# Joint pooling weights, pooled tiles stored as split, sooner input splits, and one exponential a head in a tuned encoder layer

## The chip, the cores and the metric

The kernel runs on one core of a Trainium2 chip. The core has five engines with in-order instruction queues of their own: TensorE (PE in the profile; PEld is its weight load), VectorE (DVE), ScalarE (ACT), GpSimd (POOL) and SyncE (SP), which here only issues DMA transfers. The metric is the device time of one execution, in microseconds; lower is better. Before the change it is 1769.13 us, the median of three runs (1767.67 to 1769.21).

## The reference

One encoder layer is applied to two requests with shared weights: 512 positions ("prompt") and 1024 positions ("sample"), of 1024 channels. All data are float32.

```python
a = rmsnorm(h) ; z = a @ w_in              # 1024 -> 512 q + 128 k + 128 v + 512 u
q, k = rotary(rmsnorm(q)), rotary(rmsnorm(k))   # 8 q heads, 2 k heads, of 64
o_attn = softmax(q @ k.T / 8) @ v          # every position sees all of its request
# pooling, for each of four groups of 128 channels, windows 2, 4, 8, 16:
d = window_mean(u) - u
o_pool = (d @ w_pool[group]) * pool_scale
h = h + concat(o_attn, o_pool) @ w_out     # 512 + 512 rows -> 1024
h = h + square(relu(rmsnorm(h) @ w_up)) @ w_down        # 1024 -> 4096 -> 1024
h = h + sigmoid(rmsnorm(h) @ w_ple_gate) * (p @ w_ple_proj)
y = rmsnorm(h)
```

The pooled part of the output is a product of three: d (positions x 128), w_pool (128 x 128) with its scale, and 128 rows of w_out.

## The kernel before, in words

The 1536 positions are 12 tiles of 128 (t = 0 to 11; the prompt is tiles 0 to 3) and 3 chunks of 512 (c = 0, 1, 2). Nearly every float32 operand of a matmul is **split** in two parts: a rounded high part (float32r, written by a copy) and the remainder (a subtraction). A product is then three matmuls (`three`: high-high, high-low, low-high). So every new operand costs a copy on ScalarE and a subtraction on VectorE or GpSimd. All working tiles on chip come from one pool of 49 equal slots; a slot holds 1056 numbers for each of the 128 partitions; a full tile of 1024 columns is 512 KB.

The order of instructions on TensorE, ScalarE, VectorE and GpSimd is the order of the code. Loads go through SyncE's single queue, in the order of the code too, each no earlier than the matmul issued just before it; stores stand in the same queue. A load or store that waits holds back all that are behind it.

**Stage 1, input projection** (0 to about 200 us). For each tile t, `mm_k(t, k)` runs the nine matmuls of one of the eight blocks k of 128 input channels into the PSUM tile z (two buffers). Between these steps stands everything else by hand: after k = 2 `split_x` and `stat_x` of the next x tile, after k = 3 `rotary` of the tile before (VectorE), after k = 6 `turn_qk`, which transposes the rotated q and k (PSUM tiles qp, kp), copies them to qs and ks on ScalarE, subtracts on VectorE and stores qs to DRAM (qs_d). After k = 4 a finished pooled tile goes through `pool_product`. A table `first`, keyed by (t, k), holds further work: in tiles 10 and 11 the loads of the pooling rows of w_out (wor4 to wor7), their splits (wo4 to wo7), and the first scores of attention. `pool_step` advances the window sums on GpSimd, which end in a split tile dhl for each chunk c and group g (12 in all). `pool_product` multiplies it by the split w_pool (three 512-column matmuls into py), scales and splits the result (y), and stores it to DRAM (yT_d).

The rotary uses four tables, tabq and tabk, products of the gains gq, gk and the cosines and sines (csr). GpSimd makes them at the start; GpSimd also computes the norm factor hr of each tile's heads (`rstd_of`). csr stands in the load queue behind x2 and several small constants.

**Attention** (about 200 to 560 us) is a pipeline over steps `at`; each step takes one of four heads of a unit (tile t, group g). `Unit.score` makes S (128 x 512 for the prompt, 128 x 1024 for the sample) and its row maximum nm on VectorE; `soften` the exponential on ScalarE with a running sum; `norm` the reciprocal rr on VectorE and the multiplication on GpSimd; `turn` transposes 128-column blocks of four heads (tp); `split` makes the split pt (ScalarE cast, VectorE subtraction); `weigh` multiplies with v. For the sample, `soften` makes two exponentials of 512 columns, each with its sum, and `norm` adds the two sums on VectorE first (L455):

```python
if self.nc == 2:
    ve.tensor_tensor(rr, self.sums[:, j, 0:1], self.sums[:, j, 1:2], op=ALU.add)
    ve.reciprocal(rr, rr)
```

Each step also takes one or two pieces from a list of **fillers** (`fill`): matmuls that depend on little, first the pooled part of the output projection (`pool_out`, which reads the stored pooled tiles yb and the weights wo4 to wo7, PSUM tile pp), then the heads' part (`heads_out`, po). A dictionary `extras`, keyed by the step, holds what is left of stage 1: turn_u and the rotary of tile 11 and turn_qk of tiles 10 and 11. In the later part of attention "chores" also run (`make_m`), which make the MLP's inputs on GpSimd, VectorE and ScalarE.

**MLP** (about 560 to 1560 us): seven products in place of eight for each pair of blocks (PSUM tiles px, py, pz, pq up; pd down); the sums of weight blocks made for chunk 0 are stored (kept_d) and loaded again for chunks 1 and 2. Chores between the products prepare what follows. One of them, `gating(0)`, runs near the MLP's end: for a = 0 to 3 it loads a quarter of the residual h (from hl_d), squares it and makes the split gated input hg (`gate_in`), sums the squares (`total`), and stores hg (hg_d). The generator `staged` runs the stages of the four items as a pipeline, the last stage of the oldest item first:

```python
yield from staged(range(4), fetch, square, total, keep)
```

**Gate and output** (about 1560 us to the end): products with w_ple_gate (pg) and w_ple_proj (pj), the sigmoid, the final norm and the stores.

## Time and profile before

| what | value |
|---|---|
| median of three runs | 1769.13 us (1767.67 to 1769.21) |
| the profiled execution, its own time | 1772.11 us |
| its span (first to last instruction) | 1770.3 us |
| granted clock of TensorE, mean | 0.992 |
| TensorE, matmuls: busy | 1727.3 us, 98%, 11692 instructions |
| TensorE, weight loads: busy | 1574.4 us, 89% |
| VectorE busy | 1287.1 us, 73%, 1786 instructions |
| GpSimd busy | 1078.4 us, 61%, 933 instructions |
| ScalarE busy | 906.9 us, 51%, 1730 instructions |
| DMA moved | 391.78 MB, 221 GB/s over the span |

The busy shares are means over stages with different limits, so views of single stretches are needed beside them. In the lists of groups, `out<-in` names the tile written and the tiles read, then the shapes, a count, the busy time and the mean in ns of one, and the idle time just before these instructions with what ended it. In the timeline, a row gives start, duration, engine, source line, operation and tiles, and in brackets the wait that stood ahead of it and its releaser. The clock is the share of full speed that TensorE was granted.

### The profile page before, as it was taken

What the parts mean: (1) busy time and instruction counts of PE and PEld (TensorE: products, weight loads), DVE (VectorE), ACT (ScalarE), POOL (GpSimd) and SP (SyncE); (2) the same over time, 40 slices, a digit from 0 to 9 for tenths busy, and PEclk for the clock granted to TensorE, in tenths of its full rate; (3) what the DMA queues carried; (4) which work ended last, traced back from release to release, by engine and by line L of the source; (5) the groups of instructions that cost most, each with busy time, mean ns of one, the idle gap of its engine ahead of it and who ended that gap; (6) DMA issues with size and microseconds to landing.
All of it is one profiled execution on the core that took longest, in us unless ns stands there. A gap on an engine that the chain in (4) does not pass through costs nothing. (4 is left out here: it accounts for less than half of the span.)

```text
span 1770.3 us, 31419 instructions
## 1 busy us (share of the span) xinstructions
PE 1727.3 (98%) x11692; PEld 1574.4 (89%) x11692; DVE 1287.1 (73%) x1786; ACT 906.9 (51%) x1730; POOL 1078.4 (61%) x933
## 2 busy tenths in 40 slices
...
GB/s 253 84 133 106 217 175 179 72 67 42 124 92 256 322 296 274 361 277 357 285 348 324 344 226 334 223 340 331 248 265 233 308 276 349 252 208 114 12 48 96
DMA packets 133608, 391.78 MB, mean 221 GB/s; under 512 B 14160, under 2 KB 26832, under 8 KB 133456
## 3 DMA queue, kind: packets, MB, share of 16 engines
...
HBM read 275.96 MB, written 113.77 MB: 220 GB/s over the span
## 5 line engine op out<-in xcount | busy, mean ns | idle before, releaser
L49 PE MATMUL pd<-ta,v 128*128 128x256 f32 x2688 | 339.4, 283 | 0.1
L49 PEld LDWEIGHTS pd<-ta,v 128*128 128x128 f32 x2688 | 329.6, 190 | 0.8 <-POOL v L1033 0.3
L1033 POOL TENSOR_TENSOR v<-we,v 128x512 fp32r<-128x512 f32 x128 | 184.4, 1461 | 105.7 <-DVE ta L1053 37.6
L461 POOL TENSOR_SCALAR pr<-pr,rr 128x512 f32<-128x512 f32 x160 | 111.2, 706 | 135.6 <-DVE rr L456 64.0
L49 PE MATMUL pd<-r,wd 128*128 128x512 f32 x768 | 190.5, 397 | 2.0 <-DVE r L950 2.0
L1033 POOL TENSOR_TENSOR v<-vs,v 128x512 fp32r<-128x512 f32 x96 | 128.0, 1354 | 103.6 <-DVE c L1056 37.2
L49 PE MATMUL z<-w,x 128*128 128x512 f32 (+1 forms) x864 | 175.0, 359 | 2.4 <-ACT w L159 1.1
L1053 DVE TENSOR_TENSOR ta<-c,ta 128x512 fp32r<-128x512 f32 x112 | 115.7, 1033 | 84.4 <-ACT ta L1051 77.1
L49 PEld LDWEIGHTS pd<-r,wd 128*128 128x128 f32 x768 | 140.9, 189 | 31.1 <-DVE r L950 2.8
L49 PEld LDWEIGHTS z<-w,x 128*128 128x128 f32 x864 | 142.4, 188 | 29.3 <-ACT w L159 2.8
L844 POOL TENSOR_TENSOR w<-ws,w 128x512 fp32r<-128x512 f32 x72 | 106.2, 1477 | 92.8 <-ACT w L843 88.0
L49 PE MATMUL pq<-mo,w 128*128 128x256 f32 x1152 | 153.2, 282 | 5.4 <-DMA w<-kept_d 4.2
L49 PE MATMUL pz<-mo,w 128*128 128x256 f32 x1152 | 153.6, 283 | 4.0 <-DVE u L980 3.5
L49 PE MATMUL px<-mo,w 128*128 128x256 f32 x1152 | 153.6, 283 | 0.0
L49 PEld LDWEIGHTS pz<-mo,w 128*128 128x128 f32 x1152 | 146.6, 190 | 7.7 <-DVE u L980 4.1
L49 PEld LDWEIGHTS pq<-mo,w 128*128 128x128 f32 x1152 | 143.7, 189 | 6.7 <-DVE H L1084 2.9
L49 PEld LDWEIGHTS px<-mo,w 128*128 128x128 f32 x1152 | 145.6, 191 | 1.4
L49 PE MATMUL pg<-hg,wg 128*128 128x512 f32 (+1 forms) x768 | 141.1, 338 | 0.3 <-DVE hg L1359 0.3
L49 PEld LDWEIGHTS pg<-hg,wg 128*128 128x128 f32 x768 | 119.3, 188 | 17.0 <-DVE hg L1359 0.5
L472 ACT CAST pt<-tp 128x512 fp32r<-128x512 f32 x160 | 87.7, 590 | 90.3 <-PE tp L53 88.6
L473 DVE TENSOR_TENSOR pt<-tp,pt 128x512 fp32r<-128x512 f32 x160 | 104.0, 684 | 31.4 <-ACT pt L472 31.0
L441 DVE TENSOR_REDUCE nm<-S 128x1 f32<-128x1024 f32 (+1 forms) x96 | 100.1, 1043 | 22.9 <-PE S L49 22.4
(252 smaller groups left out, 3562.2 us busy)
## 6 DMA issues: line engine op xcount, KB each, us to landing
...
```

The costliest lines, as they stand in the source:

```text
L49: last_pe[0] = nc.tensor.matmul(*a, **k).ins
L441: ve.tensor_reduce(nm, S[:, :nch * CH], axis=AX.X, op=ALU.max, negate=True)
L461: gp.tensor_scalar(p, p, rr, 1.0, op0=ALU.mult, op1=ALU.mult)
L472: sc.copy(self.pt[kt][:, 0], tp)
L473: ve.tensor_tensor(self.pt[kt][:, 1], tp, as32(self.pt[kt][:, 0]), op=ALU.subtract)
L844: gp.tensor_tensor(t[:, 1], x, as32(t[:, 0]), op=ALU.subtract)
L1033: ins = gp.tensor_tensor(lo[:, p], src[:, p], as32(hi[:, p]), op=ALU.subtract).ins
L1053: last_ve[0] = ve.tensor_tensor(t[:, 1], x, as32(t[:, 0]), op=ALU.subtract).ins
```

## The change

1. **Joint weights.** w_pool is transposed once on TensorE, scaled by pool_scale and split (`turn_pool`, in tile 3). During tiles 3 to 8 each 128 rows of w_out that belong to the pooling are loaded, split in two halves, and multiplied from the left by it (`join_load`, `join_split`, `join_product`), and the split result is stored to DRAM (`join_store` to wo_d). In tiles 10 and 11 these eight joint tiles of 512 KB are loaded (`load_joint`) in place of the four w_out row blocks, and nothing is left to split there. `pool_product` becomes `pool_store`: the split pooled tile dhl itself goes to yT_d, with no matmul.
2. **Input tiles.** `split_x` of the next tile stands after k = 0 in place of k = 2, for t > 2. The rotary tables are made on VectorE, and csr and the two gains are loaded ahead of x2. ones_sb is made at the very start.
3. **turn_qk** of tiles 10 and 11 transposes and copies k first, then q. In the attention loop, `extras` run ahead of the step's last filler, where they ran behind it.
4. **One exponential a head.** `soften` makes one exponential over all 512 or 1024 columns with one sum, `norm` a reciprocal and one multiplication. The slot of normalised scores pr holds one head of 1024 columns where it held two heads of 512.
5. **gating(0)** gets a stage `idle`, which does nothing, between fetch and square; the fetches of two further items then stand ahead of an item's square.

The core of the diff:

```diff
     n0, n1 = load_xn(0), load_xn(1)
+
+    csr = slot([P, 2, 8, 32], F32, "csr")
+    load(csr, cs)
+    tab = {}
+    for nm, g in (("q", q_g), ("k", k_g)):
+        graw = small.tile([P, HD], F32, tag="graw", name=f"g{nm}", bufs=2)
+        load(graw, g)
+        if nm == "k":
+            ve.tensor_scalar(graw, graw, 8.0, None, op0=ALU.mult)
+        tb = slot([P, 2, 8, HD], F32, f"tab{nm}")
...
     x2, n2 = load_x(2), load_xn(2)
...
     def turn_qk(t):
         c, b = t // 4, t % 4
         _, qd, kd, _ = ev.pop(t)
...
+        swap = (slice(0, HD), slice(HD, P)), (slice(HD, P), slice(0, HD))
+        kh, kl = (x[:, :, b * P:(b + 1) * P] for x in ks[c])
         qs = slot([P, 2, CH], F32R, f"qs{t}")
...
+
+        def turned_q():
+            qp = tp_ps(f"qp{t}")
+            transpose4(qp, qd)
+            return qp
+
+        def turned_k():
+            kp = tp_ps(f"kp{t}")
+            for i in range(NKV):
+                pe.transpose(kp[:, i * P:(i + 1) * P], kd[:, i * P:(i + 1) * P], id_sb)
+            return kp[:, 0:NKV * P].rearrange("p (g t) -> p g t", g=NKV)
+
+        if t < NT - 2:
+            qp, kp = turned_q(), turned_k()
+            for e, (h, _) in enumerate(swap):
+                sc.copy(qs[h, e], qp[h])
+            sc.copy(kh, kp)
+        else:
+            kp, qp = turned_k(), turned_q()
+            sc.copy(kh, kp)
+            for e, (h, _) in enumerate(swap):
+                sc.copy(qs[h, e], qp[h])
+            ve.tensor_tensor(kl, kp, as32(kh), op=ALU.subtract)
         for e, (h, l) in enumerate(swap):
             ve.tensor_tensor(qs[l, e], qp[h], as32(qs[h, e]), op=ALU.subtract)
-        ve.tensor_tensor(kl, kpv, as32(kh), op=ALU.subtract)
+        if t < NT - 2:
+            ve.tensor_tensor(kl, kp, as32(kh), op=ALU.subtract)
         sy.dma_start(qs_d[t], flat(qs))
 
...
     wpr = slot([P, 4, P], F32, "wpr")
     load(wpr, w_pool)
+    wo_d = [[dram.tile([P, D], F32, name=f"wo_d{g}{i}") for i in range(2)] for g in range(4)]
+    joint = {}
+
+    def turn_pool():
+        tp = tp_ps("wp")
+        transpose4(tp, wpr.rearrange("p a b -> p (a b)"))
+        wp = joint["w"] = slot([P, 2, CH], F32R, "wp")
+        for g in range(4):
+            part, s = slice(g * P, (g + 1) * P), psc_sb[:, g:g + 1]
+            sc.activation(wp[:, 0, part], tp[:, part], AF.Copy, scale=s)
+            ve.scalar_tensor_tensor(wp[:, 1, part], tp[:, part], s, as32(wp[:, 0, part]), op0=ALU.mult, op1=ALU.subtract)
+
+    def join_load(g):
+        joint[g] = slot([P, D], F32, f"wor{4 + g}")
+        load(joint[g], w_out[(4 + g) * P:(5 + g) * P, :])
+
+    def join_split(g, h):
+        raw = joint[g][:, h * CH:(h + 1) * CH]
+        t = joint[g, h] = slot([P, 2, CH], F32R, f"wj{g}{h}")
+        sc.copy(t[:, 0], raw)
+        gp.tensor_tensor(t[:, 1], raw, as32(t[:, 0]), op=ALU.subtract)
+
+    def join_product(g, h):
+        t, wp = joint.pop((g, h)), joint["w"]
+        pj = tp_ps(f"pj{g}{h}")
+        ws_ = [wp[:, i, g * P:(g + 1) * P] for i in range(2)]
+        for i, (w_, t_) in enumerate(three(ws_, [t[:, i] for i in range(2)])):
+            pe.matmul(pj, w_, t_, start=i == 0, stop=i == 2)
+        o = slot([P, 2, CH], F32R, f"wk{g}{h}")
+        sc.copy(o[:, 0], pj)
+        ve.tensor_tensor(o[:, 1], pj, as32(o[:, 0]), op=ALU.subtract)
+        joint[g, h, "o"] = o
+
+    def join_store(g, h):
+        o = joint.pop((g, h, "o"))
+        for i in range(2):
+            sy.dma_start(wo_d[g][i][:, h * CH:(h + 1) * CH], as32(o[:, i]))
+
+    def load_joint(g):
+        WO[4 + g] = [slot([P, D], F32R, f"wo{4 + g}_{i}") for i in range(2)]
+        for i in range(2):
+            load(as32(WO[4 + g][i]), wo_d[g][i])
 
...
-    def pool_product(c, g, dhl):
-        py = tp_ps(f"py{c}{g}")
-        for i, (w_, d_) in enumerate(three([w[:, g, :] for w in wp], [dhl[:, 0], dhl[:, 1]])):
-            pe.matmul(py, w_, d_, start=i == 0, stop=i == 2)
-        y = slot([P, 2, CH], F32R, f"y{c}{g}")
-        sc.activation(y[:, 0], py, AF.Copy, scale=psc_sb[:, g:g + 1])
-        ve.scalar_tensor_tensor(y[:, 1], py, psc_sb[:, g:g + 1], as32(y[:, 0]), op0=ALU.mult, op1=ALU.subtract)
-        sy.dma_start(yT_d[c][g], flat(y))
+    def pool_store(c, g, dhl):
+        sy.dma_start(yT_d[c][g], flat(dhl))
 
...
         def soften(self, j):
             S, nm = self.S.pop(j)
...
+            n = self.nc * CH
+            if j not in self.pr:
+                full = slot([P, D], F32, f"pr{self.id}{j}")
+                for i in range(2 // self.nc):
+                    self.pr[j + i] = full[:, i * n:(i + 1) * n]
+            sc.activation(self.pr[j], S[:, :n], AF.Exp, bias=nm, accum_out=self.sums[:, j:j + 1])
 
         def norm(self, j):
             rr = small.tile([P, 1], F32, tag="rr", name=f"rr{self.id}{j}")
-            if self.nc == 2:
-                ve.tensor_tensor(rr, self.sums[:, j, 0:1], self.sums[:, j, 1:2], op=ALU.add)
-                ve.reciprocal(rr, rr)
-            else:
-                ve.reciprocal(rr, self.sums[:, j, 0:1])
...
+            ve.reciprocal(rr, self.sums[:, j:j + 1])
+            p = self.pr[j]
+            gp.tensor_scalar(p, p, rr, 1.0, op0=ALU.mult, op1=ALU.mult)
 
         def turn(self, kt):
             tp = tp_ps(f"tp{self.id}{kt}")
-            c, b = kt // 4, kt % 4
...
+    def idle(item):
+        return iter(())
...
-    first = {(10, 6): [lambda: load_q(0)],
-             (10, 7): [lambda: load_wo(4), lambda: load_wo(5)],
-             (11, 0): [lambda: load_wo(6), lambda: load_wo(7)],
...
+    first = {(3, 4): [turn_pool],
+             (10, 6): [lambda: load_q(0)],
+             (10, 7): [lambda: load_joint(0)],
+             (11, 0): [lambda: load_joint(1)],
+             (11, 1): [lambda: unit.score(0, "tp"), lambda: load_joint(2)],
+             (11, 3): [lambda: unit.soften(0), lambda: load_joint(3)],
+             (11, 4): [lambda: load_pool(0), lambda: load_h(0, 0), lambda: unit.norm(0)],
+             (11, 5): [lambda: unit.score(1, "tp")],
              (11, 6): [lambda: load_q(1)]}
+
+    def at_join(n, act, *a):
+        first.setdefault((3 + n // KD, n % KD), []).append(lambda: act(*a))
+
+    for n in range(8):
+        g, h = divmod(n, 2)
+        if not h:
+            at_join(4 * n + 0, join_load, g)
+        at_join(4 * n + 3, join_split, g, h)
+        at_join(4 * n + 8, join_product, g, h)
+        at_join(4 * n + 14, join_store, g, h)
...
+            if k == (0 if t > 2 else 2) and t + 1 < NT:
+                split_x(t + 1, nxt[0])
             if k == 2 and t + 1 < NT:
-                split_x(t + 1, nxt[0])
...
-                pool_product(*products.pop(0)[1:])
+                pool_store(*products.pop(0)[1:])
...
-        for _ in range(n):
-            if fill and (at < 62 or at % 2 == 0 and (at < 76 or at % 3 or len(fill) > 10) or at >= 96):
+        for i in range(max(n, 1)):
+            if i == n - 1 or not n:
+                extras.pop(at, lambda: None)()
+            if n and fill and (at < 62 or at % 2 == 0 and (at < 76 or at % 3 or len(fill) > 10) or at >= 96):
                 fill.popleft()()
         fill.extend(ready)
         ready.clear()
         lag = fresh
         last = (cur, j) if cur else None
-        if at in extras:
-            extras[at]()
...
-        yield from staged(range(4), fetch, square, total, keep)
+        yield from staged(range(4), fetch, idle, square, total, keep)
```

Left out: the old place of the rotary tables (the same four products on GpSimd, behind edge_sb), ones_sb's new place, and `turn`, which now takes `self.pr[j]`.

How the rows move. First VectorE around two heads of the sample's attention (S its scores, nm its maximum, rr the reciprocal, sums the running sums of the exponential, tp and pt the transposed and the split tile, ob the finished head). Before:

```order
L441 TENSOR_REDUCE nm_01_5547<-S_01_5542 128x1
L455 TENSOR_TENSOR rr_00_5549<-sums_0_5487 128x1
L456 RECIPROCAL rr_00_5549<-rr_00_5549 128x1
L473 TENSOR_TENSOR pt_10_5568<-tp_10_5558,pt_10_5568 128x512
L473 TENSOR_TENSOR pt_11_5571<-tp_11_5563,pt_11_5571 128x512
L498 TENSOR_TENSOR ob_0_5584<-o_0_5428,ob_0_5584 64x256 x2
L441 TENSOR_REDUCE nm_02_5595<-S_02_5590 128x1
L455 TENSOR_TENSOR rr_01_5597<-sums_0_5487 128x1
L456 RECIPROCAL rr_01_5597<-rr_01_5597 128x1
```

and now:

```order
L489 TENSOR_REDUCE nm_01_5432<-S_01_5427 128x1
L503 RECIPROCAL rr_00_5434<-sums_0_5376 128x1
L516 TENSOR_TENSOR pt_10_5451<-tp_10_5441,pt_10_5451 128x512
L516 TENSOR_TENSOR pt_11_5454<-tp_11_5446,pt_11_5454 128x512
L541 TENSOR_TENSOR ob_0_5467<-o_0_5321,ob_0_5467 64x256 x2
L489 TENSOR_REDUCE nm_02_5478<-S_02_5473 128x1
L503 RECIPROCAL rr_01_5480<-sums_0_5376 128x1
```

The row that adds two sums (`rr<-sums` at L455) is gone, and the reciprocal reads sums itself; everything else keeps its order.

Next SyncE's queue where stage 1 ends and attention begins (yT_d pooled tiles in DRAM, qs_d the turned q, qb the q that attention loads, wor the raw w_out rows, wo_d the joint weights, yb the pooled tiles loaded again, y and dhl the tiles that are stored). Before:

```order
L398 DMA yT_d_0_89<-y_1882 128x1024
L56 DMA qb_1924<-qs_d_73 128x1024
L56 DMA wor_1936<-in_w_out_dram 128x1024
L345 DMA qs_d_82<-qs_1915 128x1024
L56 DMA wor_1938<-in_w_out_dram 128x1024
L56 DMA wor_1965<-in_w_out_dram 128x1024
L56 DMA wor_1967<-in_w_out_dram 128x1024
L56 DMA yb_2050<-yT_d_0_85 128x1024
L56 DMA yb_2051<-yT_d_1_86 128x1024
L398 DMA yT_d_1_90<-y_2044 128x1024
L56 DMA yb_2052<-yT_d_2_87 128x1024
L56 DMA yb_2053<-yT_d_3_88 128x1024
```

and now:

```order
L446 DMA yT_d_1_90<-dhl_1962 128x1024
L56 DMA qb_2012<-qs_d_73 128x1024
L56 DMA wo_0_2024<-wo_d_258 128x1024
L359 DMA qs_d_82<-qs_1995 128x1024
L56 DMA wo_1_2025<-wo_d_259 128x1024
L56 DMA wo_0_2053<-wo_d_260 128x1024
L56 DMA wo_1_2054<-wo_d_261 128x1024
L56 DMA wo_0_2079<-wo_d_262 128x1024
L56 DMA wo_1_2080<-wo_d_263 128x1024
L56 DMA wo_0_2115<-wo_d_264 128x1024
L56 DMA wo_1_2116<-wo_d_265 128x1024
L56 DMA yb_2131<-yT_d_0_85 128x1024
```

Eight loads of joint weights stand where four loads of w_out stood; the store of the pooled tile to yT_d_1 is now ahead of all of them, where it stood behind two of the four yb.

Last, SyncE's queue in the gating chore, near the end of the MLP (h the quarters of the residual, loaded from hl_d; hg the gated input, stored to hg_d; w_11, w_12 and we the MLP's weights). Before:

```order
L1419 DMA hg_d_6593<-hg_0_16996 128x1024
L56 DMA h_17129<-hl_d_2_6587 128x1024
L1419 DMA hg_d_6594<-hg_1_16997 128x1024
L56 DMA w_12_2_17151<-kept_d_2_396 128x1024
L56 DMA w_12_5_17176<-kept_d_5_397 128x1024
L1419 DMA hg_d_6595<-hg_0_17072 128x1024
L1419 DMA hg_d_6596<-hg_1_17073 128x1024
L56 DMA h_17213<-hl_d_3_6588 128x1024
```

and now:

```order
L56 DMA h_16834<-hl_d_1_6425 128x1024
L56 DMA h_16841<-hl_d_2_6426 128x1024
L56 DMA w_11_4_16858<-kept_d_4_400 128x1024
L56 DMA w_12_1_16909<-kept_d_1_401 128x1024
L56 DMA w_12_6_16931<-kept_d_6_402 128x1024
L56 DMA we_510_16933<-in_w_down_dram 128x2x512
L1475 DMA hg_d_6432<-hg_0_16837 128x1024
L56 DMA h_16970<-hl_d_3_6427 128x1024
```

The load of quarter 2 stood behind the store of the first hg and now comes right behind that of quarter 1; the load of quarter 3 stood behind four hg stores and now stands behind one.

63 lines of the change are left out of this document (13 added, 50 removed).

## The prediction

> **What bounds the kernel now.** I read the page's busy shares, then who TensorE waited for, then windows with the granted clock, then single places in the timeline.
>
> ```profile
> PE 1727.3 (98%) x11692; PEld 1574.4 (89%) x11692; DVE 1287.1 (73%) x1786; ACT 906.9 (51%) x1730; POOL 1078.4 (61%) x933
> ```
>
> TensorE is the bound: 98% busy, so time changes only through its own instruction count and through the stalls in its stream. "Busy" hides part of these stalls, because consecutive matmuls overlap in the record. So I need the pace of a stream without stalls.
>
> ```profile
> 1604.69 3.00 PE L49 MATMUL pd<-ta,v 128*128 128x256 f32 x24
> ...
> 1608.91 5.70 PE L49 MATMUL pg<-hg,wg 128*128 128x512 f32 x24
> ```
>
> Taking the last one's own 0.28 and 0.39 us off and dividing by 23 gives 0.118 us per 256-column matmul and 0.231 us per 512-column one. Two stretches of the second request's attention, by windows (columns: time, then busy time and instructions of PE, PEld, DVE, ACT, POOL, then clock, DMA share, GB/s) and by groups of TensorE:
>
> ```profile
> 60.00:180.00 120.00, 120.00 (x653) 103.18 (x652) 82.60 (x135) 47.83 (x93) 68.54 (x77) 1.00 0.31 112
> ...
> 330.00:420.00 90.00, 90.00 (x604) 80.75 (x603) 73.14 (x144) 60.37 (x149) 37.31 (x54) 1.00 0.14 49
> 426.00:555.00 129.00, 124.59 (x728) 98.72 (x727) 114.65 (x209) 109.25 (x260) 89.09 (x109) 1.00 0.28 101
> ```
> ```profile
> L49 PE MATMUL po<-cat,wo 128*128 128x256 f32 x243 | 34.0, 289 | 0.0
> L49 PE MATMUL o<-pt,vs 128*128 128x512 f32 x89 | 24.9, 398 | 1.0 <-DVE pt L473 1.0
> L49 PE MATMUL S<-ks,qb 128*128 128x512 f32 x88 | 24.0, 395 | 0.0
> L53 PE MATMUL tp<-id_sb,pr 128*128 128x128 f32 x184 | 23.8, 272 | 0.0
> ```
> ```profile
> L49 PE MATMUL o<-pt,vs 128*128 128x512 f32 x148 | 46.3, 422 | 2.7 <-DVE pt L473 2.2 <-ACT pt L472 0.2
> L53 PE MATMUL tp<-id_sb,pr 128*128 128x128 f32 x296 | 39.4, 274 | 1.0 <-DVE pt L473 1.0
> L49 PE MATMUL S<-ks,qb 128*128 128x512 f32 x138 | 39.1, 404 | 0.1
> L49 PE MATMUL po<-cat,wo 128*128 128x256 f32 x146 | 20.5, 289 | 0.6 <-DVE ob L498 0.6
> ```
>
> The first four groups are 330 to 420, where TensorE never idles: 243 x 0.118 + 177 x 0.231 = 69.6 us, so 184 transposes took 20.4 us, 0.111 each. The last four are 426 to 555: 146 x 0.118 + 286 x 0.231 + 296 x 0.111 = 116.2 of 129 us. There 12.8 us are lost, and VectorE is busy 89% (81% in the free stretch). That is the largest loss that this change touches.
>
> **Part by part.** The sum is made against the profiled execution: span 1770.3, time 1772.1 us, which is 3.0 above the median of the runs, 1769.1.
>
> *TensorE's work.* Twelve pool products of three 512-column matmuls go (36), eight joint products of three come (24), and four transposes: -12 x 0.231 + 4 x 0.111 = **-2.3 us**.
>
> *Rotary tables from GpSimd to VectorE, before the second x load.* In tile 2 TensorE waits twice for the rotary of tiles 0 and 1:
>
> ```profile
> 33.71 2.54 POOL L220 TENSOR_TENSOR tabq<-gq,csr 128x512 f32<-128x512 f32 x2
> ...
> 37.28 2.54 POOL L220 TENSOR_TENSOR tabk<-gk,csr 128x512 f32<-128x512 f32 x2
> ...
> 41.31 0.28 POOL L99 TENSOR_SCALAR hr<-hs 128x10 f32<-128x10 f32 x1
> 41.67 1.99 POOL L100 TENSOR_TENSOR hr<-hr,mhalf 128x10 f32<-128x10 f32 x1
> ```
> ```profile
> 43.70 0.82 DVE L292 TENSOR_TENSOR ea<-ea,hr 128x640 f32<-128x640 f32 x1 [2.35 <-POOL hr L100]
> 44.55 0.69 DVE L295 TENSOR_TENSOR ra<-ea,tabq 128x512 f32<-128x512 f32 x1
> ```
> ```profile
> 47.08 0.63 PE L53 MATMUL qp<-id_sb,eb 128*128 128x128 f32 x4 [2.49 <-DVE eb L301]
> ...
> 54.72 0.63 PE L53 MATMUL qp<-id_sb,eb 128*128 128x128 f32 x4 [1.58 <-DVE eb L301]
> ```
>
> GpSimd builds tables from 33.71 to 39.82, and hr queues behind them; without them it can start some 3 us earlier. Against that stand the 0.7 us by which the 256 KB of csr push x2 and its evacuation back, and four products of 0.69 on VectorE, which it does while waiting for x2. Rotary 0 then starts near 40.9 instead of 43.70 and is done (3.2 us later) before TensorE arrives at 44.59: -2.5. The second wait is reached at 50.65, and rotary 1 behind it ends near 51: -1.1. **-3.6 us**, bounds -4.1 and 0.
>
> *Sooner input splits, joint products in tiles 3 to 8.* TensorE is 100% busy from 60 to 180, so the sooner split gains nothing there. The added ScalarE, VectorE and GpSimd work (some 11, 7 and 11 us over 80 us) lies beside matmuls, since these engines are busy 40, 69 and 57% of that stretch. **0**, above it up to +2 if a w_out load is late.
>
> *The end of stage 1.* Before, the last product waits for VectorE, behind output-weight splits, and the clock halves after it:
>
> ```profile
> 198.91 0.93 PE L49 MATMUL py<-dhl,wp 128*128 128x512 f32 x3 [1.80 <-DVE rr L458]
> ```
> ```profile
> 20.00:30.00 10.00, 10.00 (x53) 8.50 (x52) 6.56 (x8) 6.59 (x11) 0.08 (x1) 1.00 1.01 386
> ...
> 199.80:203.20 3.40, 3.40 (x10) 2.62 (x9) 3.40 (x5) 1.47 (x3) 3.32 (x3) 0.50 0.98 327
> ```
>
> That wait is 1.80, and 3.4 us at half clock cost 1.7 more. The product and those splits are gone, but eight 512 KB loads of joint weights now stand where four stood, all ahead of the pooled tiles. From the store of dhl11 on (issued near 179) 13 transfers run up to the second pooled tile. At 386 GB/s each takes 1.36 us, so with about 3 us for the first it lands near 198; TensorE asks for it near 196 (197.1 less 1.1). A wait of 2 us on DMA replaces one of 1.8 on VectorE. **0**, bounds -3.5 (no wait, no half clock) and +4.
>
> *The last two tiles turned k first, and ahead of a filler.*
>
> ```profile
> 227.10 0.63 PE L53 MATMUL tp<-id_sb,pr 128*128 128x128 f32 x4 [1.63 <-DVE qs L343]
> ...
> 252.15 0.74 PE L49 MATMUL py<-dhl,wp 128*128 128x512 f32 x2 [0.70 <-POOL dhl L378]
> ...
> 267.16 0.63 PE L53 MATMUL tp<-id_sb,pr 128*128 128x128 f32 x4 [1.62 <-DVE qs L343]
> ```
>
> Between the k transposes and the next tp that reuses their buffer now stand four transposes and ten 512-column matmuls, 2.75 us, for a copy and a subtraction of 0.4 each: both waits go but for a few tenths, **-2.8** (bounds -3.2, 0). The product's own 0.70 goes with it: **-0.7**.
>
> *One exponential a head.* For 1024 columns the two 512-wide exponentials, two accumulator reads, the addition of the two sums and two normalisations become one of each. VectorE's addition L455, first in 330 to 420 and then in 426 to 555:
>
> ```profile
> L455 DVE TENSOR_TENSOR rr<-sums 128x1 f32<-128x1 f32 x23 | 3.8, 165 | 0.0
> ```
> ```profile
> L455 DVE TENSOR_TENSOR rr<-sums 128x1 f32<-128x1 f32 x36 | 14.8, 410 | 2.0 <-ACT pr L449 2.0
> L456 DVE RECIPROCAL rr<-rr 128x1 f32<-128x1 f32 x36 | 5.9, 164 | 1.2
> ```
>
> One element a partition takes 165 ns while GpSimd only normalises, and 410 ns once GpSimd also makes the MLP's inputs. Without it VectorE has 114.65 - 14.8 = 99.9 us of work for TensorE's 116.2, 86%. That lies between the stretch that loses nothing (81%) and this one (89%, 12.8 lost). ScalarE saves about 0.25 us a head, 9 us, and would be 86% busy too. I take 7.5 of the 12.8: **-7.5**, bounds -12.8 and -2. The Trainium skill (GPSIMD Engine Reference, "Key points") says that GpSimd contends with VectorE for SBUF where a VectorE instruction has two SBUF inputs or runs in a two-port mode; the rows above agree for the addition. Read strictly, the second half of that rule could move the stall to the reciprocal.
>
> *A gap stage in the gating chore.* One stage without work puts two loads instead of one ahead of each square:
>
> ```profile
> 1481.71 1.06 ACT L1406 ACTIVATE sqg<-h 128x1024 f32<-128x1024 f32 x1 [3.35 <-DMA h<-hl_d]
> ```
> ```profile
> 1484.59 0.69 DVE L1053 TENSOR_TENSOR ta<-c,ta 128x512 fp32r<-128x512 f32 x1 [3.93 <-POOL sqg L1413]
> ...
> 1490.94 0.41 DVE L980 TENSOR_TENSOR u<-pz,u 128x256 f32<-128x256 f32 x1
> ```
> ```profile
> 1491.40 1.86 PE L49 MATMUL pz<-mo,w 128*128 128x256 f32 x7 [3.55 <-DVE u L980]
> ```
> ```profile
> 1490.10:1496.80 6.70, 5.40 (x25) 5.40 (x26) 6.12 (x8) 0.51 (x2) 4.24 (x4) 0.50 0.75 252
> ```
>
> The last h load, issued late, holds ScalarE for 3.35 us; the cast queued behind the square feeds VectorE, whose L980 then comes 3.55 us late. The half clock makes 25 matmuls take 5.40 us instead of 2.95. With the load issued some 10 us sooner, behind one store instead of four, ScalarE goes straight on, L980 ends near 1487.6 and TensorE waits a few tenths at most: **-5.5**, bounds -6.0 and 0. On the half clock, the Trainium skill (TensorE: Matmul & The Clock Gate, Part 1) says that the gate looks at free-running windows of about 3.4 us. So the shift of the stream may decide anew whether a wait of 1.5 to 2.5 us halves the clock, which would move the sum by 1.7 either way for each.
>
> Sum: -2.3 - 3.6 - 2.8 - 0.7 - 7.5 - 5.5 = -22.4 us; 1772.1 - 22.4 = 1749.7 as a profiled execution, **1747** as a median. The matmul waits for w<-kept_d and for L950 in the MLP lie outside the change and stay.
>
> **Rivals.** (1) *Attention is not held by VectorE's load.* The chain of transpose, ScalarE cast, VectorE subtraction and the two PSUM buffers sets the pace, or the stall of 0.25 us moves to the reciprocal. For it: ScalarE is 85% busy there as well, and the waits named are for pt. Against: L456 keeps 164 ns in both stretches. Then -2 instead of -7.5: 1752.
>
> (2) *The gating wait stays.* Two L1359 of 1.8 us stretch VectorE ahead of L980, and the sooner loads delay the MLP's weights in a full DMA queue. Then 5.5 are missing: 1752.
>
> (3) *Slower: ScalarE blocks on the w_out loads in tiles 3 to 6.* Each joint split stands in ScalarE's in-order queue three matmul steps (about 5.6 us) after its load's turn, and a 512 KB load takes about that long to land. If each of four loads did what the gating load did (3.55 + 2.45 = 6 us on TensorE) and the reloads cost +4, the sum is +6: 1775. It decides only if ScalarE's delay exceeds the slack up to the next evacuation; against it stand z's two buffers and joint products five steps (over 8 us) later.
>
> (4) *The change is real but off the path:* the waits only move, and -2.3 is left: 1767.
>
> (5) *Better than forecast:* attention becomes as dense as at 330 to 420 and the end of stage 1 has no wait: -5 and -3.5, 1738.
>
> **How the numbers follow.** Forecast 0.58 (its own range 1742 to 1752), rival 1 0.16, rival 2 0.12, rival 5 0.06, rival 4 0.04, rival 3 0.04. The time is the forecast's, 1747. The range reaches from near rival 5 past rivals 1 and 2 together (1758): 1739 to 1759. A change below 0.2% (3.5 us) can't be told from none. Faster 0.92, within it 0.04, slower 0.04.
>
> **What would show it.** Right: no wait of qp over 0.6 us in tile 2; no tp wait on qs; a wait of pp on DMA of 1 to 3 us where z of tile 11 ends; VectorE under 90% between 420 and 550 and TensorE losing 3 to 7 us there; no ScalarE wait on h<-hl_d over 1 us near the end of the MLP, and full clock there. Wrong: ScalarE waiting on wor in tiles 3 to 6 with TensorE idle behind it, a wait for the joint weights above 5 us, or attention's stalls unchanged.

## The result, and the profile after

| | median | runs | ratio to before, 95% interval |
|---|---|---|---|
| before | 1769.17 us | 4 | |
| changed | 1760.05 us (1756.99 to 1761.32) | 4 | 0.9947 (0.9929 to 0.9964) |

The change makes the kernel 9.1 us faster. The forecast was 1747, 22.1 us less, with a range of 1739 to 1759; the time lies 1 us above that range. The profiled execution took 1756.99 us (span 1755.2, mean clock 0.996) against 1772.11 before, so the two traces differ by 15.1 us. The trace of before came from an execution 3 us above its median, and that of after from one 3 us below, so only 9.1 of the 15.1 belong to the change.

The engines' row of the page after:

```profile
PE 1720.7 (98%) x11684; PEld 1570.7 (89%) x11684; DVE 1253.8 (71%) x1724; ACT 889.3 (51%) x1605; POOL 1073.8 (61%) x870
```

To place the difference I took every matmul's distance to the start of the next one, less the pace of a stream without stalls (0.232, 0.119 and 0.109 us for 512, 256 and 128 columns), and summed it by stretch. The second column of each kernel is a second execution of it, profiled on another occasion.

| TensorE time lost, us | before | before, again | after | after, again |
|---|---|---|---|---|
| start to tile 3 | 9.8 | 8.2 | 5.8 | 6.3 |
| tiles 3 to 9 | -0.3 | -0.2 | **4.8** | **4.6** |
| tile 10 to the end of stage 1 | 4.5 | 4.5 | **5.6** | **6.5** |
| the prompt's attention | 5.7 | 5.6 | 4.4 | 4.4 |
| the sample's attention, to the MLP | 15.9 | 16.0 | **9.5** | **9.6** |
| MLP, chunk 0 | 4.1 | 2.2 | 1.2 | 1.9 |
| MLP, chunks 1 and 2 | 14.6 | 12.7 | 10.5 | 9.3 |
| gate and output | 6.7 | 6.8 | 6.5 | 6.5 |

Tiles 3 to 9 lost nothing before and lose almost 5 us now. That is where the joint weights are made, and the forecast had 0 there. The windows of after (same columns as in the prediction):

```profile
56.70:173.00 116.30, 113.38 (x604) 96.62 (x602) 76.21 (x131) 50.82 (x101) 76.79 (x75) 0.99 0.48 169
134.90:138.30 3.40, 3.02 (x13) 2.42 (x14) 2.37 (x6) 1.53 (x3) 3.06 (x5) 0.72 0.00 0
191.10:194.50 3.40, 3.40 (x9) 2.82 (x10) 2.16 (x3) 0.78 (x2) 3.23 (x4) 0.51 1.03 423
418.00:547.00 129.00, 127.49 (x762) 103.55 (x762) 104.89 (x181) 104.94 (x196) 82.67 (x74) 1.00 0.30 106
1477.60:1484.40 6.80, 5.63 (x45) 5.42 (x46) 6.00 (x7) 0.73 (x2) 5.48 (x4) 1.00 0.95 338
```

In the first window, tiles 3 to 9, GpSimd is busy 66% and ScalarE 44%; neither is full, and TensorE still idles 2.9 us. The next two windows show the clock at 0.72 and 0.51. The fourth is the sample's attention: 762 matmuls in 129 us where there were 728, VectorE at 81% where it had 89%. The fifth is the place of the gating wait, now at full clock. TensorE's timeline in after, the waits that bear on the steps of the prediction:

```profile
50.77 0.30 PE L53 MATMUL qp<-id_sb,eb 128*128 128x128 f32 x1 [1.00 <-DVE eb L300]
...
67.82 0.44 PE L53 MATMUL kp<-id_sb,ea 128*128 128x128 f32 x2 [0.94 <-DVE wp L373]
...
134.93 0.66 PE L53 MATMUL qp<-id_sb,eb 128*128 128x128 f32 x4 [1.63 <-DVE eb L300]
...
191.07 1.19 PE L49 MATMUL S<-ks,qb 128*128 128x512 f32 x2 [2.04 <-DMA qb<-qs_d]
...
204.93 0.47 PE L49 MATMUL pp<-yb,wo 128*128 128x512 f32 x1 [0.71 <-DMA yb<-yT_d]
...
225.95 0.44 PE L53 MATMUL qp<-id_sb,eb 128*128 128x128 f32 x2 [0.74 <-DVE pt L516]
...
1477.68 0.50 PE L49 MATMUL pz<-mo,w 128*128 128x256 f32 x2 [1.38 <-DVE u L1026]
...
1483.33 0.51 PE L49 MATMUL pq<-mo,w 128*128 128x256 f32 x2 [1.09 <-DVE c L1031]
```

The second, the third and the fourth are new. At 67.82 kp waits for a PSUM buffer that turn_pool still holds. At 134.93 TensorE waits for a rotary that is late, and the clock of 0.72 follows; its cause lies 15 us earlier, on GpSimd, ScalarE, VectorE and SyncE. There eb and ea are the two slots into which a tile's product z is copied and in which the rotary then works, ra is the rotary's scratch tile, and wj and wk are a joint tile's split rows and its result. SPq rows are SyncE's issues, idle time not marked:

```profile
117.62 1.29 POOL L383 TENSOR_TENSOR wj<-wor,wj 128x512 fp32r<-128x512 f32 x1
...
119.59 1.30 POOL L432 TENSOR_TENSOR dhl<-win,dhl 128x512 fp32r<-128x512 f32 x1
```
```profile
120.92 0.69 ACT L271 ACTIVATE eb<-z,rx 128x512 f32<-128x512 f32 x1 [1.41 <-POOL dhl L432]
```
```profile
124.78 0.82 DVE L279 TENSOR_TENSOR ra<-ea 128x640 f32<-128x640 f32 x1 [1.84 <-DMA yT_d<-dhl]
```
```profile
108.98 0.33 SPq L399 DMA_DIRECT2D wo_d<-wk  x1
...
120.92 0.33 SPq L446 DMA_DIRECT2D yT_d<-dhl  x1
121.29 2.02 SPq L399 DMA_DIRECT2D wo_d<-wk  x2
```

ScalarE's eb reads only z and rx. It does not use dhl, so the wait that the profile gives to dhl is one for a slot. All working tiles share 49 slots, handed out in the order of the code, and a freed slot goes to the next tile that asks, whose writer then waits for the last reader of the old tile. The waits tell who inherited what: eb of tile 6 got the slot of the window sums of group 2 (win), and their last reader is GpSimd's L432, which ends at 120.9. VectorE's ra of tile 6 got the slot of that pooled tile dhl itself, whose last reader is its store; this store stood at the head of SyncE's queue from 108.98 until 120.92, with the stores of the joint weights behind it. Both waits push the rotary, and TensorE pays 15 us later.

### The profile page after: what moved, and what is told of

It reads as the page before. It is cut to its first block, busy times and chain, and to the rows that moved or that the text cites. A ratio compares the mean times of both kernels' runs of the same rounds, so it can differ in the third digit from the quotient of the medians.

```text
span 1755.2 us, 31273 instructions
## 1 busy us (share of the span) xinstructions
PE 1720.7 (98%) x11684; PEld 1570.7 (89%) x11684; DVE 1253.8 (71%) x1724; ACT 889.3 (51%) x1605; POOL 1073.8 (61%) x870
## 5 line engine op out<-in xcount | busy, mean ns | idle before, releaser
L49 PE MATMUL z<-w,x 128*128 128x512 f32 (+1 forms) x864 | 179.4, 365 | 0.5 <-ACT w L159 0.3
L505 POOL TENSOR_SCALAR pr<-pr,rr 128x1024 f32<-128x1024 f32 (+1 forms) x96 | 94.5, 985 | 138.7 <-DVE rr L503 68.4
L49 PEld LDWEIGHTS z<-w,x 128*128 128x128 f32 x864 | 146.1, 193 | 27.9 <-ACT w L159 2.6
```

Of the source, the lines that this page charges most:

```text
L49: last_pe[0] = nc.tensor.matmul(*a, **k).ins
L505: gp.tensor_scalar(p, p, rr, 1.0, op0=ALU.mult, op1=ALU.mult)
```

## The experiments

Comparisons go by the ratio to the kernel before, run beside it on the same chip, since before's median itself lies between 1767.9 and 1770.0 us in these comparisons; a ratio is turned into us with 1768. The intervals are 95%. The name in brackets is used for the run further down.

**The change once more** (again), unchanged.

> The changed kernel once more, unchanged, for a second profile: what differs between two executions of one program isn't an effect of the change. If the places in which TensorE waits are set by the program alone, the same waits stand at the same places (qp near 135 us 1.6, S<-ks,qb near 191 us 2.0, the w<-kept_d waits, u near 1477 us 1.4), and only the stretches of half clock differ by multiples of about 1.7 us. If transfers set them, the w<-kept_d waits and the pd<-r,wd wait of 1.75 us that before had at 765 us come and go by 1 to 3 us. Median expected 1760, within 1.5 us.

Measured: 1757.96 us, ratio 0.9948 (0.9934 to 0.9962). The first figure holds: -9.2 us. Its lost time by stretch is the last column of the table above. The waits at 134.9 and 191 are there again, with full clock behind the second; the pooled tiles are waited for longer (2.45, where it was 0.71), and the half clock stands there (0.53 from 205.0 to 208.4):

```profile
135.25 0.44 PE L53 MATMUL qp<-id_sb,eb 128*128 128x128 f32 x2 [1.45 <-DVE eb L300]
...
191.09 0.70 PE L49 MATMUL S<-ks,qb 128*128 128x512 f32 x2 [1.74 <-DMA qb<-qs_d]
...
205.12 2.85 PE L49 MATMUL pp<-yb,wo 128*128 128x512 f32 x6 [2.45 <-DMA yb<-yT_d]
```
```profile
191.10:194.50 3.40, 3.40 (x17) 2.90 (x18) 2.64 (x4) 0.78 (x2) 3.23 (x4) 1.00 1.02 417
```

**The change without the joint weights** (no_joint). pool_product, the four w_out loads and their splits are back as they were before; everything else is the change's.

```diff
-    first = {(3, 4): [turn_pool], (10, 7): [lambda: load_joint(0)], ...
+    first = {(10, 7): [lambda: load_wo(4), lambda: load_wo(5)], ...
-                pool_store(*products.pop(0)[1:])
+                pool_product(*products.pop(0)[1:])
```

> The changed kernel without the joint weights: the twelve pool products, the four w_out loads and their splits as before, all other parts as changed. Theory: the joint weights cost more in waits (5 us from 60 to 180 us, 1 at the end of stage 1) than they take from TensorE (2.3) and from the product's wait (0.7), so this kernel is about 3 us faster than the changed one, near 1757, with no TensorE idle time over 0.3 us between 60 and 180 us. Rival (the prediction's sum): the joint weights are worth 3 us, and this kernel is 3 us slower than the changed one, near 1763; the stalls between 60 and 180 us then come from the sooner input splits or the rotary tables and stay.

Measured: 1753.16 us, ratio 0.9920 (0.9907 to 0.9933). Without its largest part the change is better: the joint weights cost 5.0 us (0.0028 of 1768; some 3.4 either way if the two intervals are taken as independent). Tiles 3 to 9 lose -0.1 us and TensorE has no stall there, though the input splits stand as early as in the change; the splits are therefore not what costs:

```profile
57.00:165.00 108.00, 108.00 (x587) 92.67 (x586) 70.95 (x123) 43.66 (x85) 66.56 (x67) 1.00 0.34 122
```

**The store not before its turn** (hold_store). The store of a pooled tile may be issued no earlier than the matmul issued just before it, as loads are. In the kernel before, the store had the same place in the program, but it followed a product on TensorE, which timed it.

```diff
     def pool_store(c, g, dhl):
-        sy.dma_start(yT_d[c][g], flat(dhl))
+        ins = sy.dma_start(yT_d[c][g], flat(dhl)).ins
+        tc.add_manual_dep(ins, last_pe[0].name, NOSYNC, reason="not before its turn")
```

> The changed kernel, with the store of a pooled tile issued no earlier than its turn in the program (as loads are), not as soon as the queue's order allows. Theory A: the 5 us lost between 60 and 180 us, and the wait for qb at 191 us, come from these stores: SyncE stands on one of them until GpSimd has finished the tile (120.9 us), the joint-weight stores and the loads behind it are late, and VectorE's ra of tile 6 has been given the slot of that very tile and waits for its landing at 124.70 us. Then both waits go (qp near 135 us: 1.6 and 1.7 of half clock; S<-ks,qb near 191 us: 2.0 and 1.7 of half clock); the loads of yb gain only some 2 us, so pp waits about 2 us for them instead of 0.7. Sum about -5 us against the changed kernel, near 1755. Rival B: the added joint work itself (VectorE's instructions take up to twice as long there while GpSimd runs) makes the rotary late. Then the wait of qp near 135 us stays at 1 us or more and only the queue's part at 191 us moves: -1 to -2 us.

Measured: 1755.03 us, ratio 0.9934 (0.9922 to 0.9946), 2.5 us better than the change, with intervals that overlap. Loss in tiles 3 to 9 is 2.6 where it was 4.8. Slots are now handed out in another order, and by its wait win's slot went to a joint tile wj, which ScalarE wrote 1.96 us late; the wait for the rotary shrank from 1.63 to 0.97, and no half clock followed it, which is 1.7 of the 2.2 us gained:

```profile
121.72 0.62 ACT L382 CAST wj<-wor 128x512 fp32r<-128x512 f32 x1 [1.96 <-POOL dhl L432]
...
135.11 0.55 PE L53 MATMUL qp<-id_sb,eb 128*128 128x128 f32 x3 [0.97 <-DVE eb L300]
...
201.14 0.70 PE L49 MATMUL pp<-yb,wo 128*128 128x512 f32 x2 [2.19 <-DVE vs L275]
```

The wait for qb at 191 is gone, as the qb load no longer stands behind a store that waits for GpSimd: it was issued at 173.19 here, in after at 185.19, right behind a store at 184.76 whose pooled tile GpSimd finished at 184.74. But TensorE now reaches the pooled part sooner than its tiles and pp waits 2.19 instead. (The bracket names vs, which ended at 201.0; the first pooled tile landed at that moment too.) So the store explains part, and the wait on GpSimd is not the store's.

**And GpSimd's added work taken away** (hold_vector). Stores held as in hold_store, and the eight subtractions of the joint split go to VectorE.

```diff
         sc.copy(t[:, 0], raw)
-        gp.tensor_tensor(t[:, 1], raw, as32(t[:, 0]), op=ALU.subtract)
+        ve.tensor_tensor(t[:, 1], raw, as32(t[:, 0]), op=ALU.subtract)
```

> The kernel with held stores (1755.0 us), and the low half of the raw w_out rows (wj) subtracted on VectorE, not on GpSimd: eight subtractions fewer on GpSimd (1.3 us each), eight more on VectorE. Theory A': what makes the rotary of tile 6 late is GpSimd, which finishes the pooled tile too late; tiles of ScalarE and VectorE that are given its slot or that of its window sums wait for it (in the held kernel ScalarE stood 1.96 us ahead of wj for the pooled tile of GpSimd at 121.7 us). Then the qp wait near 135 us (0.97) and the half clock behind it go, some 1.5 us: 1753.5. Rival: VectorE itself is too full there; its eight more subtractions make the qp wait longer, 1756 or more. The wait of 0.94 at 68 us (a PSUM buffer of the turned w_pool) stays either way.

Measured: 1757.36 us, ratio 0.9930 (0.9917 to 0.9944): no gain over hold_store that the interval could tell, where 1.5 us were expected. GpSimd is done 1.6 us sooner than in hold_store, and yet ScalarE idles 5.36 us for it, some 2 us longer than it idles at this place in after (3.39, for TensorE's qp). By this wait the slot fell to a tile that is written sooner, qs of tile 5. The wait of qp near 135 is gone, and TensorE's pj waits 1.20 for ScalarE's eb instead:

```profile
120.16 1.17 ACT L347 CAST qs<-qp 64x512 fp32r<-64x512 f32 x2 [5.36 <-POOL dhl L432]
```

GpSimd's load is therefore not the cause by itself: who inherits the slot, and when that one needs it, decides.

**The slot released late** (late_release). The kernel of hold_store, and win of this one group is touched again (eight columns multiplied by 1.0 on GpSimd) when its pooled tile is stored, at least six steps later. So the next tile to ask gets another slot.

```diff
-    def pool_store(c, g, dhl):
+    def pool_store(c, g, dhl, cur):
+        if (c, g) == (0, 2):
+            gp.tensor_scalar(cur[:, PAD:2 * PAD], cur[:, PAD:2 * PAD], 1.0, 1.0, op0=ALU.mult, op1=ALU.mult)
```

> The kernel with held stores, and the window sums of chunk 0, group 2 touched once more on GpSimd (8 columns, by 1.0) when that tile's store has its turn, so that the slot of these sums is given away only later; no work is taken from any engine. Theory A'': it is this one slot. GpSimd is the last to read it (pooled tile, about 120 to 122 us), and whichever tile was given it waited: eb of tile 6 on ScalarE in the changed kernel (to 120.9), wj of the last half on ScalarE with held stores (1.96 us, to 121.7), qs of tile 5 on ScalarE with the subtraction on VectorE (to 120.1). Then no instruction of ScalarE waits for the pooled tile here, the qp wait near 135 us (0.97 with held stores) is under 0.3, and TensorE loses 1.0 to 1.5 us in tiles 3 to 9 (the wait for the turned w_pool near 68 us) where it lost 2.6: 1 to 2 us faster than with held stores (ratio 0.9934), 0.9925. Rival: the slots are short as such; another tile waits in its place and the loss stays at 2 us or more.

Measured: 1752.98 us, ratio 0.9914 (0.9900 to 0.9928), 6.0 us better than the change (0.9948). GpSimd ends L432 no sooner than in after (119.91 + 1.30), and nobody on ScalarE waits for it; the rotary is in time, if only just: VectorE is done with eb at 133.60, after 3.01 us of waiting for GpSimd's norm factors hr, and TensorE takes eb at 133.65:

```profile
119.75 0.69 ACT L271 ACTIVATE eb<-z,rx 128x512 f32<-128x512 f32 x1
...
119.91 1.30 POOL L432 TENSOR_TENSOR dhl<-win,dhl 128x512 fp32r<-128x512 f32 x1
```
```profile
133.65 0.66 PE L53 MATMUL qp<-id_sb,eb 128*128 128x128 f32 x4
...
200.55 0.70 PE L49 MATMUL pp<-yb,wo 128*128 128x512 f32 x2 [2.95 <-DMA yb<-yT_d]
```

So of the 4.8 us lost in tiles 3 to 9, 3.2 come from inherited slots and the store: 2.2 went with the held store, 1.7 of them half clock, and 1.0 with the slot released late. The late release was not run without the held store. The 1.6 us still lost are mostly two waits of kp, 0.9 and 0.4, for PSUM buffers that turn_pool and a joint product hold. The wait for the pooled tiles at 200.55 stays at 2.95.

**The weights loaded sooner, with and without joint weights** (joint_early, early_w_out). Two kernels: late_release with the joint weights' loads four or five steps earlier and the pooled tiles' load two steps earlier; and no_joint with the w_out loads and their splits moved ahead by two to four steps.

```diff
+             (10, 3): [lambda: load_joint(0)],
+             (10, 4): [lambda: load_joint(1)],
+             (10, 5): [lambda: load_q(0), lambda: load_joint(2)],
+             (10, 6): [lambda: load_joint(3)],
+             (11, 2): [lambda: load_pool(0)],
```

> The kernel with the late release, and the eight joint weights loaded from tile 10's fourth step on (3 to 6 steps sooner), the pooled tiles of chunk 0 two steps sooner. What is open: whether the joint weights themselves are worth their 2.3 us of TensorE once their waits are gone. The late release still loses 5.3 us around the end of stage 1 (pp waits 2.95 for yb, half clock behind it). If only the place of the loads in the queue does that, the wait shrinks below 1 us, and this kernel is 3 us faster than the late release (ratio 0.9914), near 0.9895, and no slower than the kernel with split w_out loaded sooner (0.9903). Rival: eight loads of 512 KB where four stood simply take that long; the wait moves to the joint weights or to qb, and the ratio stays at 0.991 or above.

> The kernel without the joint weights (ratio to before 0.9920), its four w_out loads issued in tile 10 two to four steps sooner, split two to three steps sooner, and the pooled tiles of chunk 0 loaded two steps sooner. If the end of stage 1 is held by VectorE's splits of w_out (py waits 1.9 there, about 1.5 of half clock behind it) and the late yb, both go: -3 to -4 us, ratio 0.990. Rival: the sooner copies stand in ScalarE's queue ahead of the evacuation of tile 10 and wait there for loads or slots, as the joint weights did: no gain or a loss.

Measured: joint_early 1752.42 us, early_w_out 1751.89 us, both ratios 0.9903 (0.9887 to 0.9919). Both are faster than both kernels of this case: by ratio 17 us faster than before and 8 us faster than the change. joint_early was expected near 0.9895; its gain over late_release, 1.9 us, is within the intervals. The waits at the end of stage 1, first with joint weights (2.95 before the move), then without (no_joint's product waited 1.89 there):

```profile
202.08 0.50 PE L49 MATMUL pp<-yb,wo 128*128 128x512 f32 x1 [0.56 <-DMA yb<-yT_d]
```
```profile
195.73 0.50 PE L49 MATMUL py<-dhl,wp 128*128 128x512 f32 x1 [0.66 <-DVE y L411]
```

The length of the program from tile 3 to the sample's first score, from the matmul records, holds all of the joint work and little else that differs:

| before | no_joint | after | after, again | hold_store | late_release | joint_early | early_w_out |
|---|---|---|---|---|---|---|---|
| 251.5 | 249.4 | 253.9 | 254.7 | 250.7 | 250.3 | 247.4 | 247.6 |

After is 4.5 to 5.3 us longer than no_joint, which agrees with the 5.0 of the medians. With the waits at the end of stage 1 mostly gone on both sides the two are equal (247.4 and 247.6): the 2.3 us of products that joint weights save are lost again around them, 1.6 of it in tiles 3 to 9. By the medians no gain from joint weights can be told here; their intervals of some 2.8 us either way would not exclude one of 2.3.

**One exponential a head alone** (one_exp), in before: `soften`, `norm` and `turn` as in the change, nothing else.

```diff
-            for c in range(self.nc):
-                sc.activation(self.pr[j // 2, c][:, j % 2], S[:, c * CH:(c + 1) * CH], AF.Exp, ...)
+            sc.activation(self.pr[j], S[:, :n], AF.Exp, bias=nm, accum_out=self.sums[:, j:j + 1])
```

> The kernel before with the one-exponential part alone. The prediction's term is -7.5 us; the two profiles show 6.4 us less lost on TensorE from 320 to 600 us. Expected about -6.5 against the kernel before, near 1762.5. Rival 1 of the prediction (the chain of transpose, cast and subtraction sets the pace, not VectorE's load): -2, near 1767.

Measured: 1761.87 us, ratio 0.9968 (0.9956 to 0.9980): -5.7 us. The sample's attention loses 9.4 us instead of 15.9, and the window is that of after, to the matmul:

```profile
420.00:549.00 129.00, 127.51 (x763) 103.62 (x762) 105.06 (x181) 104.96 (x197) 82.82 (x75) 1.00 0.29 106
```

**The addition put back** (add_back). The change, with a dead addition of one element a partition on VectorE ahead of each reciprocal of the sample. Exponential and normalisation stay single.

```diff
+            if self.nc == 2:
+                ve.tensor_tensor(rr, self.sums[:, j:j + 1], mhalf[:, 0:1], op=ALU.add)
             ve.reciprocal(rr, self.sums[:, j:j + 1])
```

> The changed kernel with VectorE's one-element addition back ahead of each reciprocal of the sample's heads (64 of them; its result is overwritten at once), all else of the one-exponential part as changed. The prediction's reason: this addition, 410 ns where GpSimd makes the MLP's inputs, is what fills VectorE. Then most of the 6.4 us come back: +4 to +6 against the changed kernel, and TensorE loses some 14 to 16 us between the first of the sample's scores and the MLP, as before (15.9; 9.5 in the changed kernel). Rival: the gain comes from ScalarE (one exponential and one accumulator read fewer a head) and GpSimd (one instruction for two); then at most +1.5, and the loss stays near 10 us.

Measured: 1762.15 us, ratio 0.9961 (0.9946 to 0.9977), some 2.3 us slower than the change by ratio, less than the 4 to 6 expected and with intervals that overlap. In the profile the sample's attention loses 13.8 us: 4.2 of the 6.4 gained there are gone again. The stretch of add_back as a window and by groups, and the reciprocal's group of after:

```profile
422.00:551.00 129.00, 125.50 (x742) 100.61 (x741) 113.92 (x214) 103.27 (x194) 80.20 (x72) 1.00 0.28 102
```
```profile
L504 DVE TENSOR_TENSOR rr<-sums,mhalf 128x1 f32<-128x1 f32 x37 | 10.8, 293 | 0.5 <-ACT pr L499 0.5
L505 DVE RECIPROCAL rr<-sums 128x1 f32<-128x1 f32 x37 | 6.1, 164 | 1.3
```
```profile
L503 DVE RECIPROCAL rr<-sums 128x1 f32<-128x1 f32 x37 | 5.7, 155 | 1.4 <-ACT pr L499 1.3
```

Eleven us of an addition on VectorE whose result nobody uses cost TensorE 4.2. The addition also delays the reciprocal behind it, but no wait of TensorE in this window names the scores that the reciprocal normalises; 2.4 us of its waits name VectorE's pt, as 3.2 did in before and 0.4 in after. The addition takes 293 ns here, 410 in before and 165 where GpSimd only normalises; the reciprocal keeps 155 to 164 throughout. The Trainium skill (GPSIMD Engine Reference, "Key points") has contention of VectorE with GpSimd for instructions with two SBUF inputs, and these three numbers agree: the addition has two and is stretched, the reciprocal has one and is not.

**The idle stage alone** (idle_stage), in before.

```diff
-        yield from staged(range(4), fetch, square, total, keep)
+        yield from staged(range(4), fetch, idle, square, total, keep)
```

> The kernel before with the gap stage in the gating chore alone. The prediction's term is -5.5 us (a wait of 3.55 and half clock behind it go), its rival 2 expects 0. In the profiles of the changed kernel 2.4 us are still lost on TensorE there (pz 1.4 and pq 1.1, at full clock); a kernel without the stage lost 3.1 at full clock. Expected from that: -0.7, and up to 2.4 more in those executions in which the old wait halves the clock; about -1.5 in the median.

Measured: 1765.33 us, ratio 0.9977 (0.9968 to 0.9986): -4.1 us, where -1.5 was expected. TensorE's first wait behind the gating chore and the clock behind it:

```profile
1488.04 0.51 PE L49 MATMUL pz<-mo,w 128*128 128x256 f32 x2 [1.40 <-DVE u L983]
```
```profile
1488.00:1491.40 3.40, 3.36 (x28) 3.36 (x29) 3.40 (x2) 0.00 (x0) 3.03 (x2) 1.00 0.93 308
```

The wait is not gone but 1.40 long, a second of 1.08 follows, and the clock behind them is full. In after ScalarE's square starts without a wait, and VectorE sets the rest, in this order:

```profile
1466.21 1.06 ACT L1462 ACTIVATE sqg<-h 128x1024 f32<-128x1024 f32 x1
```
```profile
1471.47 2.32 DVE L1084 TENSOR_TENSOR vs<-we,vs 128x1024 f32<-128x1024 f32 x1
1473.70 1.79 DVE L1415 SCALAR_TENSOR_TENSOR hg<-h,gple_sb,hg 128x512 fp32r<-128x512 f32 x1
1475.41 1.22 DVE L1130 TENSOR_TENSOR H2u<-pd,H2u 128x1024 f32<-128x1024 f32 x1
1476.54 0.74 DVE L1415 SCALAR_TENSOR_TENSOR hg<-h,gple_sb,hg 128x512 fp32r<-128x512 f32 x1
1477.20 0.42 DVE L1026 TENSOR_TENSOR u<-pz,u 128x256 f32<-128x256 f32 x1
```

Four instructions of 6.1 us stand ahead of the one that TensorE waits for: the chore's own (L1415) and others that run then. What the stage is worth depends on the execution it is held against: counted as in the table above, TensorE loses in the last 90 us ahead of the gate 7.0 and 5.5 us in the two profiles of before, 4.5 and 4.2 in one_exp and tables, which lack the stage too and show full clock there, and 3.6 to 3.9 in the eleven profiles of kernels that have it.

**The kernel before once more** (before_again), unchanged, a single execution.

> The kernel before once more, unchanged, for a second profile. The first took 1772.1 us, 4 above the median of all its runs on this chip (1767.9). If the prediction's sum was made against an unlucky execution, this profile shows smaller waits for pd<-r,wd near 765 us (1.75 there) and pz<-mo,w near 1491 us (3.55), or full clock behind them, and a span near 1766; if these are fixed by the program, they stand as before.

Measured: 1766.84 us, where the first profile had 1772.11. Two places of this second trace, the one in the gating chore and one in MLP chunk 0 that the change does not touch, and the window behind each; then the place in chunk 0 in the first trace of before, wait and window:

```profile
763.80 0.50 PE L49 MATMUL pd<-r,wd 128*128 128x512 f32 x1 [1.42 <-DVE r L950]
...
1486.94 0.50 PE L49 MATMUL pz<-mo,w 128*128 128x256 f32 x2 [2.90 <-DVE u L980]
```
```profile
763.80:767.20 3.40, 3.40 (x18) 2.89 (x19) 2.79 (x4) 3.40 (x8) 2.30 (x2) 1.00 0.54 217
...
1487.00:1490.40 3.40, 3.40 (x21) 3.40 (x22) 3.40 (x4) 0.00 (x0) 0.94 (x2) 0.68 0.94 276
```
```profile
765.63 0.74 PE L49 MATMUL pd<-r,wd 128*128 128x512 f32 x2 [1.75 <-DVE r L950]
```
```profile
765.60:769.00 3.40, 3.37 (x9) 2.66 (x10) 2.31 (x3) 3.40 (x8) 2.26 (x2) 0.62 0.53 216
```

The wait at the same place was followed by full clock here and by 0.62 there, 18 matmuls against 9. In the gating chore the wait is 2.90 here, not 3.55, and 3.4 us of half clock lie behind it, not 6.7. So the base of the sum held half-clock stretches that come and go, among them half of what the gating term priced.

**The rotary tables alone** (tables), in before: made on VectorE, csr and the gains loaded ahead of x2, ones_sb early.

```diff
     n0, n1 = load_xn(0), load_xn(1)
+    csr = slot([P, 2, 8, 32], F32, "csr")
+    load(csr, cs)
...
-            gp.tensor_tensor(
+            ve.tensor_tensor(
```

> The kernel before with the rotary tables on VectorE and csr ahead of x2 (and ones_sb made at the start) alone. The prediction's term is -3.6. In five profiles with this part the two qp waits of tile 2 are 0 and 1.0, in four without it 1.3 to 2.5 and 1.6: -2 to -3 us expected. Rival: the later x2 only moves the loss, within 0.7 us of before.

Measured: 1765.53 us, ratio 0.9983 (0.9971 to 0.9994): -3.0 us. The first wait in tile 2 (2.49 in the first profile of before, 1.34 in the second) is gone, the second keeps 1.00 of its 1.58, as in after:

```profile
44.48 0.60 PE L53 MATMUL qp<-id_sb,eb 128*128 128x128 f32 x4
...
51.51 0.63 PE L53 MATMUL qp<-id_sb,eb 128*128 128x128 f32 x4 [1.00 <-DVE eb L301]
```

**The old turn of the last two tiles** (no_joint_old_turn), in no_joint: turn_qk turns q first everywhere, `extras` run behind the step's fillers.

```diff
-            if i == n - 1 or not n:
-                extras.pop(at, lambda: None)()
...
+        if at in extras:
+            extras[at]()
```

> The kernel without the joint weights (1753.2 us), and the last two tiles turned q first again, behind the filler, as in the kernel before. The prediction's term for the new turn is -2.8. In the profile of the kernel without the joint weights the two tp waits of 1.63 and 1.62 are gone, and one wait of 0.98 for pt stands in their place: about 2.3 us slower, 1755.5. Rival: the waits only change their names, within 0.7 us of 1753.2.

Measured: 1757.88 us, ratio 0.9932 (0.9920 to 0.9945), against 0.9920 with the new order: the new turn is worth 2.1 us, with intervals that overlap. Both tp waits return (the second at 263.87, 1.63 us). The second fence shows the one wait of another kind that no_joint has in their place (0.74 in after):

```profile
224.09 0.41 PE L53 MATMUL tp<-id_sb,pr 128*128 128x128 f32 x2 [1.62 <-DVE qs L342]
```
```profile
220.45 0.44 PE L53 MATMUL qp<-id_sb,eb 128*128 128x128 f32 x2 [0.98 <-DVE pt L482]
```

## Why the prediction was right and wrong

The direction was right, the size was not. The terms of the sum beside what each part measured, the first three alone in before, the turn and the joint weights by leaving them out of a kernel that has the rest:

| step | forecast, us | measured, us |
|---|---|---|
| one exponential a head | -7.5 | -5.7 (-7.8 to -3.5) |
| gap stage in the gating chore | -5.5 | -4.1 (-5.7 to -2.5) |
| rotary tables | -3.6 | -3.0 (-5.1 to -1.1) |
| the last two tiles' turn | -2.8 | -2.1 |
| joint weights: products -2.3, product's wait -0.7, tiles 3 to 8 and the end of stage 1 0 | -3.0 | **+5.0** |
| sum | -22.4 | -9.9; the whole change -9.2 |

**The step that failed** is "lies beside matmuls, since these engines are busy 40, 69 and 57% of that stretch: 0". It cost 4.9 us in tiles 3 to 9 (4.8 lost in after, -0.1 in no_joint), and the busy shares after the change, 44, 66 and 66%, give no sign of it. The step looked for a full engine or a late load. What decided was shared resources that no busy share shows. The larger part, 3.2 us, was slots whose last reader had got later, GpSimd for one and a store that waited for GpSimd for the other, given to tiles that another engine needed at once, with 1.7 us of half clock behind the wait. Against hold_store, late_release moved only the one slot's release and took the rest of that wait away with GpSimd no faster. The smaller part, some 1.3 us, was PSUM buffers that turn_pool and the joint products hold while kp needs one.

**The end of stage 1**, put at 0 with bounds -3.5 and +4, was mis-sized within its bounds: 3.8 us lost in no_joint, 5.6 and 6.5 in after. The named wait came (pp on yb, 0.71 and 2.45 in the two profiles), but ahead of it stood one that I had not listed, of the scores for qb (2.04, with the clock at 0.51 behind it, and 1.74), because the qb load stands in SyncE's queue behind the pooled tile's store. It stood behind such a store before, too, but one that was issued at 178.83, when VectorE had written y; the store of dhl waited for GpSimd until 184.74. With -2.3 for the products this gives 4.9 + 1.8 to 2.7 - 2.3 = +4.4 to +5.3, the +5.0 measured.

**Rival 3**, ScalarE held up in tiles 3 to 8 by the joint work, was right about the engine, the tiles and the sign of the joint work's term, and wrong about the reason and the size. ScalarE did wait for three of the wor loads (2.04, 0.88 and 1.28 us, 4.2 in all), but TensorE's three waits in these tiles (0.94, 1.63 and 0.35 us) name other work, so the slack that the rival's condition spoke of held.

**One exponential** was right in mechanism. VectorE's 104.89 us stand against 120.8 of TensorE's own work in the window (129 less 8.2 lost), 87% where the forecast worked out 86 from L455's duration, and the addition by itself carries 4.2 of 6.4 us in the profile. The size was 1.8 too large. Rival 1 (-2) lies outside the interval, and its stall did not move to the reciprocal. The remaining 2.2 of 6.4 were not separated further; the single accumulation and normalisation are what is left.

**The gating chore**: ScalarE's wait for h went, as forecast, and no half clock stood behind it; but that half clock was missing in two kernels without the stage as well, so it was no lasting part of the price. Not right either was "waits a few tenths at most": 1.38 and 1.09 remained, with one L1415 of 1.79 and one of 0.74 ahead of L1026, which is rival 2's place and part of its size. The profiles show 0.3 to 3.4 us for the stage, so the -4.1 is not shown to be its own. Part of it is clock: the mean over the runs was 0.9957 against 0.9940, which is 3 us of 1768, and how much of that this stage caused is open.

**Tables and turn** came out at 83 and 75% of their terms; the second rotary wait kept 1.00 where the step had it ending near 51, and new waits of 0.7 to 1.2 on pt took the place of the tp waits; the tables' first wait, priced at 2.5, was 1.34 in the second profile of before.

**The base.** Subtracting 3 us for the profiled execution was right as to the time. But the terms were priced from waits and clocks of that one execution, and the second trace shows shorter ones. 8.0 of the 13.2 us missed are the joint weights, 1.8 and 1.4 the two largest other terms, 1.3 the turn and the tables; the last 0.7 is what the parts measured one by one do not add up to.
